# Copying the value products' whole accumulator side out of PSUM on ScalarE, and adding its halves on VectorE from SBUF

## The chip, the core and the metric

The kernel runs on one core of a Trainium2 chip. The engines named below are TensorE (PE in the profile, with its weight loads listed apart as PEld), VectorE (DVE), ScalarE (ACT), GpSimd (POOL) and SyncE (SP, which issues DMA transfers). TensorE writes its products to PSUM; the other engines read them from there or work in SBUF. The metric is the device time of one execution in microseconds.

## What is computed

One step of a hybrid decoder layer: a prompt of 1024 tokens and 8 single-token samples go through one input projection, stick-breaking attention with 16 heads of 64 channels, a state-space branch, gates, an output projection and a layer norm. The change lies in the prompt's attention, which is, cut to its core:

```python
z = jnp.einsum("bqhd,bkhd->bhqk", q, k) * (HEAD_DIM ** -0.5) + sb_bias
causal = k_pos[None, :] < q_pos[:, None]
log_beta = jax.nn.log_sigmoid(z)
log_keep = jnp.where(causal, log_beta - z, 0.0)
log_w = log_beta + lax.cumsum(log_keep, axis=3, reverse=True) - log_keep
w = jnp.where(causal, jnp.exp(log_w), 0.0)
o = jnp.einsum("bhqk,bkhd->bqhd", w, v)
...
y_att = (o * jax.nn.silu(g_att)) @ w_att_out
```

A weight w of query t and key s is beta(t, s) times the product of (1 - beta) over the keys between s and t; so the keys need a running product instead of a softmax.

## The kernel before

Heads are worked on in 8 pairs. While the attention of pair p runs, TensorE also computes the input projection of pair p + 1 (line 142, 344 columns at a time, each product three times with values split in a high and a low part), and GpSimd prepares tables for the state-space branch (lines 495 to 510). The order of TensorE's instructions is written out by the program: a list of attention steps, with projection matmuls woven in between by an assumed cost for each step. The other engines' order comes from the scheduler when the program is built; every engine then works through its own list in order and waits on semaphores.

For a head h of a pair, the queries are taken in four blocks m of 256 (two of 128 each), in the order m = 3, 0, 2, 1. For a block:

- `scores` (lines 661 to 673): TensorE makes q.k for 128 queries (z, in PSUM). ScalarE makes keep = sigmoid(-z) (ke, line 662) and beta = sigmoid(z) (be, line 663). VectorE makes the running product over the keys with a scan (line 672), and multiplies it into beta (line 673).
- `turn` (lines 690 to 694): TensorE transposes the weights of two key blocks (tp, in PSUM). ScalarE copies them out rounded as the high part (wthi, or wdhi on the diagonal, line 693), and VectorE makes the low part (wtlo, wdlo, line 694).
- `values` (line 707), two turns later (LAG = 2): TensorE multiplies with the values. The stationary operand holds the values' high part in 64 columns and their low part in the other 64, so that the result has the high part's products in partitions 0 to 63 and the low part's in 64 to 127. Four matmuls go with each turn: high, low, high, low part of the weights.

When a block's last turn is in, its result has to be read: the two halves of the partitions are added, the sum is multiplied by the attention gate, silu(g) (sg), and sent to DRAM. The accumulator is one tile `o` of PSUM with two sides of 256 columns, used by turns:

```python
self.acc, self.side = ps.tile([128, 2, 256], F32, tag="o", bufs=1, name="o"), 0
```

The first matmul of a block waits for the reading of the block just before it. That holds although the blocks alternate sides: both sides are one tile. There are 8 pairs, 2 heads and 4 blocks, so 64 such readings. In the lines that read, `own` is the half of the partitions that belongs to head h, 0 to 63 for h = 0 and 64 to 127 for h = 1. Line 714 (ScalarE) copies the low half out, line 715 (VectorE) adds the high half from PSUM, line 716 (VectorE) multiplies by the gate, line 717 sends. `high_priority` moves instructions ahead in the scheduler's choice.

Of the kernel before, what the change touches and what calls it, by code (L numbers as in the profile page):

```python
# [13 lines left out]
ALU = mybir.AluOpType  # L14
# [70 lines left out]
def blk(i, w=128):  # L85
    return slice(w * i, w * i + w)
# [454 lines left out]
class Attention:  # L541
# [155 lines left out]
    def values(self, p, h, m, j, hi, lo):  # L697

        k, nc, pool, st = self.k, self.k.nc, self.pool, self.st[p]
        first, last = ORDER[m][0], ORDER[m][-1]  # L700
        if j == first:
            self.side = 1 - self.side
        o = self.acc[:, self.side]
        for a in range(2):
            v, at = st["v"][h][:, 2 * j + a], 2 * a if j < m else 2 - 2 * a
            for t in (hi, lo):
                nc.tensor.matmul(o, v, t[:, at:at + 2].rearrange("p a b -> p (a b)"),  # L707
                                 start=(j == first and a == 0 and t is hi), stop=(j == last and a == 1 and t is lo))
        if j != last:
            return  # L710
        own = slice(64 * h, 64 * h + 64)
        x = pool.tile([128, 256], F32, tag="ox", bufs=3, name="ox")
        with k.tc.high_priority(HURRY):
            nc.scalar.copy(x[own], o[64:128])
            nc.vector.tensor_tensor(x[own], o[0:64], x[own], ALU.add)
        nc.vector.tensor_tensor(x[own], x[own], st["sg"][own, blk(m, 256)], ALU.mult)  # L716
        k.q["A"].dma_start(k.d_a[p][own, blk(m, 256)], x[own])

# [1001 lines left out]
```

## Time and profile before

| | us |
|---|---|
| median of 3 runs | 1667.35 (1664.79 to 1669.0) |
| profiled execution | 1668.55 |
| its span | 1666.5 |
| PE busy in it | 1497.7 (90%) |
| DVE busy | 1265.3 (76%) |
| POOL busy | 895.0 (54%) |
| ACT busy | 754.0 (45%) |

The span is the time from the first to the last instruction in the profiled execution. The busy time of an engine counts its instructions, not its waits. The values in a row of the timeline are the start, the duration, the engine, the line, the operation, what it writes and reads with their sizes (partitions x columns), and how many alike are put together; a bracket at the end tells how long the engine had been idle before and what ended that. An instruction of DVE or ACT can be listed as starting a little before its predecessor ends.

### The profile page before, as it was taken

How to read it: one execution, taken by the hardware profiler on the slowest of the kernel's cores; microseconds unless marked ns; L12 is line 12 of the kernel's file. 1: busy time of each engine (PE TensorE's matmuls, PEld its weight loads, DVE VectorE, ACT ScalarE, POOL GpSimd, SP SyncE). 2: the span in 40 equal slices, each digit the busy share in tenths (PEclk: the TensorE clock that was granted, in tenths of full speed). 3: DMA queues.
4: the chain of work that ended last, by engine and by line, in shares of the span. 5: the costliest groups of instructions: out<-in, count | busy, mean ns of one | idle time of the engine just before them, and what ended most of it. 6: DMA issues, size and time to landing. Idle time of an engine off the chain costs nothing.

```text
span 1666.5 us, 26016 instructions
## 1 busy us (share of the span) xinstructions
PE 1497.7 (90%) x9257; PEld 1423.4 (85%) x9257; DVE 1265.3 (76%) x2342; ACT 754.0 (45%) x1380; POOL 895.0 (54%) x744
## 2 busy tenths in 40 slices
PE   4899899999999999999989898987988869999997
PEld 3799898989898989899978888887878869999885
DVE  8748888888888888872688878978559994544566
ACT  4466666666676666663333333333352222321200
POOL 3437676767676767664456555456336542122154
PEclk8899999999999999999999999889989989999998
DMA  9233333333333333326689888768355576754322
GB/s 333 71 100 82 81 81 81 81 81 81 82 81 82 81 81 81 81 88 205 214 274 292 261 256 266 256 200 233 113 181 172 188 266 240 250 182 150 105 89 89
DMA packets 164125, 258.72 MB, mean 155 GB/s; under 512 B 45049, under 2 KB 106233, under 8 KB 163867
## 3 DMA queue, kind: packets, MB, share of 16 engines
q1 hardware_dynamic: 137945, 163.62, 32.5%
q0 software_dynamic: 23456, 84.95, 15.9%
q10 hardware_dynamic: 2594, 8.49, 1.9%
q8 instruction: 73, 1.20, 0.3%
q14 instruction: 57, 0.47, 0.1%
HBM read 188.38 MB, written 57.86 MB: 148 GB/s over the span
## 4 chain that ended last, share of the span: by engine, by line
PE 41%; DVE 25%; issue 8%; DMA 5%; ACT 4%; POOL 2%; SPq 0%; DVEq 0%; ACTq 0%; POOLq 0%
PE pj L142 26%; PE f L1403 6%; DVE l_t L895 4%; DVE s_sc L837 3%; DVE ke L672 3%; PE o L707 3%; PE tp L690 2%; DMA s_t<-in_cache_k,s_idx 2%; PE z L661 2%; DVE vs L643 2%; DVE be L673 2%; DVE s_t L832 1%; DMA w<-in_w_in 1%; DVE m L1255 1%; DVE ox L716 1%
## 5 line engine op out<-in xcount | busy, mean ns | idle before, releaser
L142 PE MATMUL pj<-ahi,whi 128*128 128x344 f32 x2112 | 700.9, 333 | 56.9 <-ACT u L981 20.4
L142 PE MATMUL pj<-alo,whi 128*128 128x344 f32 x2112 | 691.3, 329 | 10.3 <-DVE alo L1231 5.8
L142 PE MATMUL pj<-ahi,wlo 128*128 128x344 f32 x2112 | 585.0, 329 | 14.2 <-POOL wlo L110 14.2
L142 PEld LDWEIGHTS pj<-ahi,whi 128*128 128x128 f32 x2112 | 410.3, 194 | 65.6 <-ACT u L981 21.4
L142 PEld LDWEIGHTS pj<-alo,whi 128*128 128x128 f32 x2112 | 410.5, 194 | 15.3 <-DVE alo L1231 6.9
L142 PEld LDWEIGHTS pj<-ahi,wlo 128*128 128x128 f32 x2112 | 385.0, 193 | 17.6 <-POOL wlo L110 15.8
L672 DVE TENSOR_TENSOR_SCAN ke<-ke,eye 128x896 f32<-128x896 f32 (+7 forms) x128 | 214.2, 1674 | 81.9 <-ACT ke L662 81.5
L110 POOL TENSOR_TENSOR wlo<-w,whi 128x1024 fp32r<-128x1024 f32 x53 | 134.2, 2532 | 242.7 <-ACT whi L109 242.4
L109 ACT CAST whi<-w 128x1024 fp32r<-128x1024 f32 x90 | 94.9, 1055 | 162.0 <-PE pj L142 111.3
L662 ACT ACTIVATE ke<-z,nhb 128x448 f32<-128x448 f32 (+2 forms) x192 | 112.0, 583 | 82.6 <-PE z L661 79.2
L673 DVE TENSOR_TENSOR be<-be,ke 128x896 f32<-128x896 f32 (+7 forms) x128 | 128.3, 1003 | 11.7 <-DVE ke L672 0.5
L837 DVE SCALAR_TENSOR_TENSOR s_sc<-s_t,s_q,s_sc 128x512 f32<-128x512 f32 x126 | 112.4, 892 | 22.0 <-issue 9.9
L663 ACT ACTIVATE be<-z,hb 128x448 f32<-128x448 f32 (+2 forms) x192 | 110.7, 577 | 0.0
L816 POOL DMA_INDIRECT s_t<-in_cache_k,s_idx x64 | 71.3, 1114 | 39.8 <-issue 12.8
L690 PE MATMUL tp<-ident,be 128*128 128x128 f32 x576 | 89.4, 273 | 0.0
L495 POOL TENSOR_TENSOR pr<-tab 128x256 f32<-128x256 f32 x32 | 31.1, 972 | 102.4 <-DMA tab<-d_tab 98.8
L693 ACT CAST wthi<-tp 128x512 fp32r<-128x512 f32 x96 | 56.6, 590 | 54.7 <-PE tp L690 52.6
L895 DVE SCALAR_TENSOR_TENSOR l_t<-l_t,l_sc 128x128 f32<-128x128 f32 x256 | 78.5, 366 | 2.3 <-DMA l_t<-in_cache_v,l_idx 2.3
L496 POOL TENSOR_TENSOR pt<-tab 128x256 f32<-128x256 f32 x64 | 77.8, 1216 | 3.1
L574 POOL TENSOR_TENSOR sg<-sg,zg 128x1024 f32<-128x1024 f32 x8 | 22.0, 2746 | 99.2 <-ACT sgs L573 99.2
L1525 ACT ACTIVATE gate<-pj 128x344 f32<-128x344 f32 x72 | 33.0, 459 | 92.2 <-PE pj L142 90.1
L661 PE MATMUL z<-kl,qs 128*128 128x448 f32 (+2 forms) x192 | 66.7, 348 | 3.0 <-DMA kl<-kl 3.0
(320 smaller groups left out, 2865.6 us busy)
## 6 DMA issues: line engine op xcount, KB each, us to landing
w<-in_w_in SPq DMA_DIRECT2D x38, 512.0 KB
w<-in_w_in POOLq DMA_DIRECT2D x26, 512.0 KB
wc<-in_w_cond SPq DMA_DIRECT2D x24, 512.0 KB
gst<-d_gg SPq DMA_DIRECT2D x8, 576.0 KB
x<-in_xr SPq DMA_DIRECT2D x9, 512.0 KB
xt<-in_xt SPq DMA_DIRECT2D x8, 516.0 KB
d_ma<-gate SPq DMA_DIRECT2D x8, 516.0 KB
d_mm<-gate SPq DMA_DIRECT2D x8, 516.0 KB
```

The source lines that it names most:

```text
L109: nc.scalar.copy(whi, w32)
L110: self.eng.tensor_tensor(wlo, w32, whi.bitcast(F32), ALU.subtract)
L142: PE.matmul(ps[c], w[:, blk(t)], x[:, cs(c)], start=(t == 0 and i == 0), stop=(t == KT - 1 and i == 2))
L661: nc.tensor.matmul(z[:, 0:wide], st["q", h][:, blk(i)], x[:, s:s + wide], start=j == 0, stop=j == 1)
L662: nc.scalar.activation(ke[:, s:s + cw], z[:, 0:cw], AF.Sigmoid, bias=k.nhb[:, hd:hd + 1], scale=-0.125)
L663: nc.scalar.activation(be[:, s:s + cw], z[:, 0:cw], AF.Sigmoid, bias=k.hb[:, hd:hd + 1], scale=0.125)
L672: nc.vector.tensor_tensor_scan(rev, rev, self.eye[:, NP - n:][:, ::-1], 0.0, ALU.mult, ALU.add)
L673: nc.vector.tensor_tensor(be, be, ke[:, 1:n + 1], ALU.mult)
L690: PE.transpose(tp[:, 2 * order[a] + e], w[e][:, blk(2 * j + a)], k.ident)
L837: DVE.scalar_tensor_tensor(sc, t, q[:, d - d0:d - d0 + 1], sc, op0=ALU.mult, op1=ALU.add)
L895: nc.vector.scalar_tensor_tensor(t[:, d], t[:, d], 1.0, self.sc, op0=ALU.mult, op1=ALU.mult, accum_out=self.acc[:, j, 8 * c + d:8 * c + d ...
L1403: PE.matmul(pp[c], a[:, token(i)], w[:, blk(c, 512)], start=(t == 0 and a is ah and w is wh), stop=(t == KT - 1 and a is al))
```

## The change

ScalarE copies all 128 partitions of the accumulator's side, and not only its lower products; VectorE then adds the two halves of this copy in SBUF, and no longer reads PSUM. The addition is also taken out of the block with the raised priority.

```diff
         own = slice(64 * h, 64 * h + 64)
         x = pool.tile([128, 256], F32, tag="ox", bufs=3, name="ox")
         with k.tc.high_priority(HURRY):
-            nc.scalar.copy(x[own], o[64:128])
-            nc.vector.tensor_tensor(x[own], o[0:64], x[own], ALU.add)
+            nc.scalar.copy(x, o)
+        nc.vector.tensor_tensor(x[own], x[0:64], x[64:128], ALU.add)
         nc.vector.tensor_tensor(x[own], x[own], st["sg"][own, blk(m, 256)], ALU.mult)
         k.q["A"].dma_start(k.d_a[p][own, blk(m, 256)], x[own])
```

The order of the instructions is the same on every engine in the two programs; what changes is which of them wait for what. On TensorE, at the first value products of the second block (m = 0) of the first pair's first head, the program of before has these rows (the bracket names the engines whose counts are waited for):

```order
L707 MATMUL o<-wdhi,vs 128x256 [waits DVE_49]
L707 MATMUL o<-wdlo,vs 128x256
```

and the changed program these:

```order
L707 MATMUL o<-wdhi,vs 128x256 [waits Activation_49]
L707 MATMUL o<-wdlo,vs 128x256 [waits DVE_49]
```

The first matmul's wait on VectorE for line 715 of the block before (m = 3) has become one on ScalarE for line 714; and the second matmul now has a wait on VectorE of its own, for wdlo of line 694, which line 715's wait covered before.

On VectorE, where the result of that block m = 0 is read, before:

```order
L672 SCALAR_TENSOR_TENSOR ke_636<-ke_636,eye 128x1024 [waits Activation_49]
L715 TENSOR_TENSOR ox<-o,ox 64x256 [waits Activation_49]
L673 TENSOR_TENSOR be<-be,ke_636 128x1024 [waits DVE_49]
L694 TENSOR_TENSOR wdlo<-tp,wdhi 128x384 [waits Activation_49]
L716 TENSOR_TENSOR ox<-ox,sg 64x256 [waits DVE_49]
```

and changed:

```order
L672 SCALAR_TENSOR_TENSOR ke_636<-ke_636,eye 128x1024 [waits Activation_49]
L715 TENSOR_TENSOR ox<-ox 64x256 [waits Activation_49]
L673 TENSOR_TENSOR be<-be,ke_636 128x1024 [waits DVE_49]
L694 TENSOR_TENSOR wdlo<-tp,wdhi 128x384 [waits Activation_49]
L716 TENSOR_TENSOR ox<-ox,sg 64x256
```

Line 715 keeps its place. Line 716 needs no wait on its own engine any more, because the wait of line 673 now reaches up to line 715.

## Rows read from the trace of the kernel before

**Rows 1.** Busy time by stretch: length, then PE, PEld, DVE, ACT, POOL; granted clock.
```profile
125.00:770.00 645.00, 604.54 (x4001) 583.54 (x4001) 547.69 (x607) 429.94 (x857) 445.06 (x395) 0.98 0.32 83
...
423.00:443.00 20.00, 17.00 (x106) 15.85 (x106) 18.71 (x20) 12.21 (x27) 11.55 (x11) 0.91 0.41 103
443.00:464.00 21.00, 20.93 (x143) 20.56 (x142) 17.86 (x21) 15.02 (x30) 14.46 (x14) 1.00 0.17 49
```

**Rows 2.** Waits, 125 to 770 us: total us, times, longest us.
```profile
PEld o L707 <- DVE ox L715: 34.9, 32, 2.9
...
PEld o L707 <- DVE wtlo L694: 13.3, 7, 2.2
```

**Rows 3.** Timeline of PE's weight loads, 430 to 444 us: start, us, instruction, idle before.
```profile
431.16 0.19 PEld L707 LDWEIGHTS o<-wdhi,vs 128*128 128x128 f32 x1 [2.11 <-DVE ox L715]
...
437.77 0.19 PEld L707 LDWEIGHTS o<-wthi,vs 128*128 128x128 f32 x1 [1.34 <-DVE ox L715]
```

**Rows 4.** ACT's instructions by shape, 125 to 770 us: count, busy us, mean ns.
```profile
L714 ACT COPY ox<-o 64x256 f32<-64x256 f32 x64 | 23.6, 369 | 34.4 <-PE o L707 32.8
...
L571 ACT COPY sg<-pj 128x336 f32<-128x336 f32 x7 | 3.0, 432 | 0.0
```

**Rows 5.** Timeline of ACT, 425 to 433 us.
```profile
425.40 0.37 ACT L714 COPY ox<-o 64x256 f32<-64x256 f32 x1
```

**Rows 6.** Timeline of DVE, 423 to 448 us.
```profile
423.67 2.33 DVE L672 TENSOR_TENSOR_SCAN ke<-ke,eye 128x896 f32<-128x896 f32 x1 [0.97 <-ACT ke L662]
...
434.39 2.88 DVE L672 TENSOR_TENSOR_SCAN ke<-ke,eye 128x1024 f32<-128x1024 f32 x1
437.30 0.42 DVE L715 TENSOR_TENSOR ox<-o,ox 64x256 f32<-64x256 f32 x1
437.75 0.56 DVE L694 TENSOR_TENSOR wdlo<-tp,wdhi 128x384 fp32r<-128x384 f32 x1
...
440.66 0.68 DVE L694 TENSOR_TENSOR wtlo<-tp,wthi 128x512 fp32r<-128x512 f32 x1
...
443.47 0.42 DVE L715 TENSOR_TENSOR ox<-o,ox 64x256 f32<-64x256 f32 x1 [0.53 <-ACT ox L714]
```

**Rows 7.** Timeline of PE, 397 to 401 and 440 to 443 us.
```profile
400.25 0.39 PE L707 MATMUL o<-wtlo,vs 128*128 128x256 f32 x1 [1.91 <-DVE wtlo L694]
...
440.73 0.28 PE L707 MATMUL o<-wdlo,vs 128*128 128x256 f32 x1
...
442.33 0.28 PE L707 MATMUL o<-wtlo,vs 128*128 128x256 f32 x1
```

**Rows 8.** Lines 715 and 716: least, median and longest ns, first and last start.
```profile
L715 DVE TENSOR_TENSOR ox<-o,ox x64: 386/414/419, 140.8 to 765.5; 64x256 f32<-64x256 f32 x64
...
L716 DVE TENSOR_TENSOR ox<-ox,sg x64: 403/423/2153, 142.7 to 765.9; 64x256 f32<-64x256 f32 x64
```

**Rows 9.** Timeline of DVE, 384 to 402 us.
```profile
384.96 2.02 DVE L672 TENSOR_TENSOR_SCAN ke<-ke,eye 128x896 f32<-128x896 f32 x1 [2.46 <-ACT ke L662]
386.90 0.39 DVE L715 TENSOR_TENSOR ox<-o,ox 64x256 f32<-64x256 f32 x1
387.22 1.25 DVE L673 TENSOR_TENSOR be<-be,ke 128x896 f32<-128x896 f32 x1
...
392.14 0.39 DVE L715 TENSOR_TENSOR ox<-o,ox 64x256 f32<-64x256 f32 x1
...
394.16 2.15 DVE L716 TENSOR_TENSOR ox<-ox,sg 64x256 f32<-64x256 f32 x1
```

**Rows 10.** Timeline of POOL, 384 to 402 us.
```profile
385.17 2.35 POOL L497 TENSOR_TENSOR pi<-pi,pt 128x256 f32<-128x256 f32 x1
...
390.14 2.55 POOL L496 TENSOR_TENSOR pt<-cc,tab 128x288 f32<-128x288 f32 x1
...
392.77 3.27 POOL L587 TENSOR_TENSOR qs<-z,qs 64x1024 fp32r<-64x1024 f32 x1
396.11 0.87 POOL L497 TENSOR_TENSOR gi<-gi,pt 128x288 f32<-128x288 f32 x1
```

## The prediction

> **What bounds the kernel now.** I read the busy time by stretch first, then the waits, then the timeline of one head pair, 372 to 454 us; the other pairs repeat it. All 64 instances of the changed lines run in the attention stage. There, from 125 to 770 us, the reader sees TensorE (PE) busy 604.5 of 645.0 us and VectorE (DVE) 547.7 [rows 1]: PE is the longer queue, DVE is not far behind, so a wait taken from PE can come back as another wait for DVE.
>
> The waits name the line that changes: PE's weight loads (PEld) stood idle 34.9 us, 32 times, until L715 had ended, and 13.3 us, 7 times, until L694 [rows 2]. The reason is the order on DVE. L715 stands behind a scan (L672) of up to 2.88 us [rows 6], and the next value products (L707) may not write into the accumulator's bank until L715 has read it. In the pair shown the loads wait 2.11 us at 431.16 and 1.34 us at 437.77, 3.45 us together [rows 3]. Eight pairs of that are 27.6 us; the 7.3 us that are left of the list are short waits, 0.9 us a pair.
>
> **The change part by part.** *The wait goes to ScalarE.* L714 now releases the bank. In front of the 2.11 us wait it had ended at 425.40 + 0.37 = 425.77 us, 5.4 us before L715 let PE go on [rows 3, 5]. It now copies 128 partitions instead of 64, with as many columns. Its price lies between 369 ns (today's mean) and 432 ns (128x336 from PSUM: all 128 partitions and more columns) [rows 4]; I take 369, since the 63 ns between the two have 80 more columns to account for. Either end is far below those 5.4 us. PE's direct gain is up to 34.9 us.
>
> *What is late next.* The second matmul of each L707 group reads wtlo or wdlo, which DVE makes at L694. DVE's run from 423.67 to 443.47 us shows no idle time [rows 6], so an earlier PE does not make it earlier. Inside it, wdlo is ready at 437.75 + 0.56 = 438.31 and wtlo at 440.66 + 0.68 = 441.34 us, and PE reads them at 440.73 and 442.33 [rows 6, 7]. The spare is 2.42 and then 0.99 us. Of the 3.45 us that PE gains in front of them it has to give back all but 0.99; that much stays, since DVE next waits for ACT (0.53 us idle at 443.47) and ACT for PE. Of the short waits I keep half, 0.45 us a pair, because two further L715 of a pair meet GpSimd work and sit right in front of an L694. Kept: 0.99 + 0.45 = 1.44 us a pair, times 8 is 11.5 us. Its bounds are 0 and 34.9.
>
> *L715 from SBUF.* It becomes an instruction like L716: 64x256, both inputs in SBUF. L715 took at most 419 ns, L716 up to 2153, with medians of 414 and 423 [rows 8]. The timeline tells why: L716 at 394.16 lay beside a GpSimd (POOL) tensor_tensor that ran from 392.77 to 396.04 and ended 0.27 us behind it, while L715, with one input in PSUM, passed beside POOL's at 386.90 and 392.14 in 0.39 us [rows 9, 10]. The price of one L715 lies between 0 and 2.15 - 0.42 = 1.73 us. I price these two as L716, done 0.28 us behind the POOL instruction that they meet: POOL ends at 385.17 + 2.35 = 387.52 and at 390.14 + 2.55 = 392.69, so L715 ends at 387.80 and not 387.29, and at 392.97 and not 392.53 [rows 9, 10]. That is 0.51 and 0.44 us.
>
> [...]
>
> *Two small losses in order.* The program now lets L673 behind L715 wait for L715 and not for the scan alone (the order rows show L716's own wait on DVE gone for that). Today L673 starts 0.07 us before L715 has ended (387.22 against 387.29) [rows 9]. And L715 now reads two halves of the partitions: where its output lies in the lower half, it starts today 0.08 us before the scan has ended (386.90 against 386.98), where it lies in the upper, 0.03 behind (437.30 against 434.39 + 2.88) [rows 6, 9]. I take 0.03 behind for both: 0.11 for L715 and 0.10 for L673, twice, 0.42 us a pair. Bounds: 0 and twice that.
>
> Both L715 of this stretch lie in a DVE run from 384.96 to beyond 400 us that ends in the L694 for which PE already waits 1.91 us at 400.25 [rows 7, 9]. So all of it comes out on PE: 0.51 + 0.44 + 0.42 = 1.37 us a pair, times 8 is 11.0 us. Bounds: 0, and 8 x 2 x 1.73 = 27.7.
>
> **The sum.** -11.5 + 11.0 = -0.5 us on the profiled execution's 1668.55 us (span 1666.5 and 2.05 around it), which lies 1.2 above the median of the three runs, 1667.35. I give the forecast on the median: 1666.9 us. What the stage gains or loses I carry to the end undiminished, as PE is the queue that goes through it.
>
> **The rivals.** *Faster: POOL hardly touches L715* (chance 0.23). For it: the POOL instructions that L715 meets are themselves drawn out by the scan in front (2.35 and 2.55 us; one of their kind took 0.87 at 396.11 [rows 10]), so they may end sooner than their rows say. Then 0.42 x 8 = 3.4 us stand against 11.5 (15.1 with the short waits kept whole): 8 to 12 us faster, 1656 to 1659. Within it, with 0.02, DVE gives way altogether and the full 34.9 come: 1632; the spares of 2.42 and 0.99 us speak against it.
>
> *Slower, by a GpSimd instruction that slips in* (0.20). L673 used to stand ready while L715 ran. Now it waits for L715's end, and by then POOL's next tensor_tensor is already waiting and goes first; L673 waits for it as L716 did. One such instruction takes 0.87 us [rows 10]; two a pair in 8 pairs are 13.9 us: 1681. It decides once more than 0.3 us per instance come in this way (16 x 0.3 = 5). Against it: POOL then has that work behind it and hinders DVE less later in the same run. [...]
>
> *Slower, by the clock* (0.15). [...]
>
> **How the numbers follow.** What a measurement of this kernel can tell from no change is 0.3%, 5 us. The forecast, chance 0.42, with its own range from 1662 to 1672, is no change. Faster by more: 0.23. Slower by more: 0.20 + 0.15 = 0.35. The range from 1657 to 1680 takes in most of the faster rival and the lower part of the slower ones, and leaves out 2 in 10.
>
> **What would show it.** Right: no wait of PE for L715; in its place longer waits for L694 (13.3 us on PEld becoming some 44: 11.0 more at places like 400.25, and 8 x 2.46 given back at places like 438 and 441); the two L715 of a pair that meet POOL at 0.8 to 1 us; L714 at 370 ns. Wrong: L715 at 0.42 us throughout (then the faster rival), L673 grown by more than L715 (POOL first), or a granted clock below 1 in the busy stretch behind 443 us of a pair (the clock). If PE's idle time in the stage falls by over 10 us, the claim that DVE takes back the gain is wrong.

## The result, and the profile after

The changed kernel takes 1681.8 us (median of 7 runs, 1674.15 to 1683.79) against 1666.35 us before (7 runs): ratio 1.0088, 95% interval 1.0069 to 1.0107. It is slower by 15 us. The forecast was no change, 1666.9 us, and the range ended at 1680. The profiled execution took 1683.79 us, span 1682.0.

The attention stage first. The stretch is drawn out to 790 us because the stage ends later; columns as in [rows 1], then PE's waits as in [rows 2]:

```profile
125.00:790.00 665.00, 608.03 (x3997) 590.71 (x3996) 568.92 (x607) 427.90 (x857) 456.11 (x394) 0.97 0.31 80
```

```profile
PEld o L707 <- DVE wtlo L694: 34.9, 15, 4.1
...
PEld tps L621 <- DVE wtlo L694: 17.6, 7, 2.7
...
PEld o L707 <- DVE wdlo L694: 7.8, 10, 1.2
```

The wait for L715 is gone from the list, all 34.9 us of it. In its place stand 60.3 us of waits for L694, where there had been 13.3 [rows 2]. 17.6 us of them are on a line that did not wait before at all, L621. VectorE needs 568.92 us for the 607 instructions that took 547.69 [rows 1]: 21.2 us more for the same work.

Where on VectorE? The groups by shape (count, busy us, mean ns, idle before), and the two lines' least, median and longest:

```profile
L715 DVE TENSOR_TENSOR ox<-ox 64x256 f32<-64x256 f32 x64 | 44.2, 690 | 5.0 <-ACT ox L714 3.1
L716 DVE TENSOR_TENSOR ox<-ox,sg 64x256 f32<-64x256 f32 x64 | 36.2, 566 | 1.1
...
L673 DVE TENSOR_TENSOR be<-be,ke 128x1024 f32<-128x1024 f32 x15 | 29.8, 1988 | 0.3
```

```profile
L715 DVE TENSOR_TENSOR ox<-ox x64: 420/670/2490, 140.7 to 786.0; 64x256 f32<-64x256 f32 x64
L716 DVE TENSOR_TENSOR ox<-ox,sg x64: 404/423/2150, 143.5 to 786.4; 64x256 f32<-64x256 f32 x64
```

L715's median went from 414 to 670 ns [rows 8], and its last instance from 765.5 to 786.0 us: the stage ends 20.5 us later, of which some 5 are made up behind it. L673 of 128x1024 takes 1988 ns on the mean, though nothing in it was edited; before it was

```profile
L673 DVE TENSOR_TENSOR be<-be,ke 128x1024 f32<-128x1024 f32 x15 | 19.5, 1297 | 0.1
```

One pair shows why. These are VectorE and GpSimd in the stretch that answers to [rows 9, 10], some 6 us later than there:

```profile
391.36 2.51 DVE L672 TENSOR_TENSOR_SCAN ke<-ke,eye 128x896 f32<-128x896 f32 x1 [1.95 <-ACT ke L662]
393.90 0.79 DVE L715 TENSOR_TENSOR ox<-ox 64x256 f32<-64x256 f32 x1
394.72 1.46 DVE L673 TENSOR_TENSOR be<-be,ke 128x896 f32<-128x896 f32 x1
...
399.35 0.73 DVE L715 TENSOR_TENSOR ox<-ox 64x256 f32<-64x256 f32 x1
400.12 3.31 DVE L673 TENSOR_TENSOR be<-be,ke 128x1024 f32<-128x1024 f32 x1
...
403.81 0.54 DVE L716 TENSOR_TENSOR ox<-ox,sg 64x256 f32<-64x256 f32 x1
404.28 2.60 DVE L672 TENSOR_TENSOR_SCAN ke<-ke,eye 128x128 f32<-128x128 f32 x1
...
409.08 0.68 DVE L694 TENSOR_TENSOR wtlo<-tp,wthi 128x512 fp32r<-128x512 f32 x1
```

```profile
399.88 2.46 POOL L587 TENSOR_TENSOR qs<-z,qs 64x1024 fp32r<-64x1024 f32 x1
```

L715 ends at 400.08, and L673 starts 0.04 us later. But GpSimd's L587 was already up, at 399.88; it runs until 402.34, and L673 ends at 403.43. In the kernel before these were VectorE's rows at the same place, between those of [rows 9]:

```profile
392.45 1.32 DVE L673 TENSOR_TENSOR be<-be,ke 128x1024 f32<-128x1024 f32 x1
...
396.24 1.02 DVE L672 TENSOR_TENSOR_SCAN ke<-ke,eye 128x128 f32<-128x128 f32 x1
```

There L673 started 0.08 us ahead of the end of L715 (392.45 against 392.53); L587 was up only at 392.77 [rows 10] and met L716 instead. From the start of the scan at 391.36 to the end of wtlo at 409.76 are 18.40 us; the same run of instructions took 384.96 to 400.19, 15.23 us. I call this run A (first head of a pair: from the 128x896 scan to the wtlo behind the 128x128 product). PE stands at its end:

```profile
403.95 0.39 PE L707 MATMUL o<-wdlo,vs 128*128 128x256 f32 x1 [0.97 <-DVE wdlo L694]
409.82 0.39 PE L707 MATMUL o<-wtlo,vs 128*128 128x256 f32 x1 [3.86 <-DVE wtlo L694]
...
443.54 0.49 PE L621 MATMUL tps<-ident,zs 128*8 128x128 f32 x3 [2.50 <-DVE wtlo L694]
```

The 1.91 us wait of [rows 7] has become 3.86, with 0.97 in front of it. Behind it TensorE's granted clock was 0.66 on the mean (0.50 from 412 to 414 us, 1.00 again from 415 us), while PE was busy throughout (columns as in [rows 1]):

```profile
410.00:415.00 5.00, 5.00 (x26) 4.94 (x27) 3.74 (x7) 2.49 (x5) 0.00 (x0) 0.66 0.78 206
```

At 443.54 the 2.11 us of [rows 3] are back, as 2.50 us, on L621. The transposes of sample_rows write into a buffer of the turned weights, and cannot start before L694 has read it. In the profile before, these two rows (VectorE, PE) show that they had 0.41 us to spare, 432.24 - (431.14 + 0.69):

```profile
431.14 0.69 DVE L694 TENSOR_TENSOR wtlo<-tp,wthi 128x512 fp32r<-128x512 f32 x1
```

```profile
432.24 0.55 PE L621 MATMUL tps<-ident,zs 128*8 128x128 f32 x3
```

### The profile page after: what moved, and what is told of

Read it like the earlier page. It is cut to its first block, busy times and chain, and to the rows that moved or that the text cites. A ratio compares the mean times of both kernels' runs of the same rounds, so it can differ in the third digit from the quotient of the medians.

```text
span 1682.0 us, 26015 instructions
## 1 busy us (share of the span) xinstructions
PE 1501.7 (89%) x9257; PEld 1431.1 (85%) x9257; DVE 1291.7 (77%) x2342; ACT 752.5 (45%) x1380; POOL 904.7 (54%) x744
## 4 chain that ended last, share of the span: by engine, by line
PE 48%; DVE 25%; DMA 7%; issue 7%; ACT 5%; SPq 2%; POOL 2%; DVEq 0%; ACTq 0%; POOLq 0%
PE pj L142 32%; PE f L1403 6%; DVE ke L672 4%; DVE l_t L895 4%; DVE be L673 3%; PE o L707 3%; PE z L661 2%; PE tp L690 2%; DVE vs L643 2%; DMA w<-in_w_in 1%; DVE ox L715 1%; DVE s_sc L837 1%; DMA d_g<-yy 1%; DVE wtlo L694 1%; DVE ox L716 1%
## 5 line engine op out<-in xcount | busy, mean ns | idle before, releaser
L673 DVE TENSOR_TENSOR be<-be,ke 128x896 f32<-128x896 f32 (+7 forms) x128 | 134.0, 1047 | 12.2 <-ACT wthi L693 0.5
L663 ACT ACTIVATE be<-z,hb 128x448 f32<-128x448 f32 (+2 forms) x192 | 110.8, 577 | 0.0
L816 POOL DMA_INDIRECT s_t<-in_cache_k,s_idx x64 | 70.0, 1093 | 38.9 <-issue 12.5
L495 POOL TENSOR_TENSOR pr<-tab 128x256 f32<-128x256 f32 x32 | 27.0, 844 | 116.6 <-DMA tab<-d_tab 112.9
L707 PE MATMUL o<-wtlo,vs 128*128 128x256 f32 x192 | 52.7, 296 | 31.2 <-DVE wtlo L694 31.0
L496 POOL TENSOR_TENSOR pt<-tab 128x256 f32<-128x256 f32 x64 | 78.7, 1229 | 3.1
```

Source lines behind the costliest of these rows:

```text
L663: nc.scalar.activation(be[:, s:s + cw], z[:, 0:cw], AF.Sigmoid, bias=k.hb[:, hd:hd + 1], scale=0.125)
L673: nc.vector.tensor_tensor(be, be, ke[:, 1:n + 1], ALU.mult)
```

## The experiments

Theory H, formed on this: the sum of two SBUF inputs that lie in different partitions makes VectorE stop twice, in front of L715 and behind it, and GpSimd's tensor_tensor gets in at these stops. A stop means that an instruction starts a little behind the end of the one in front, and not ahead of it; the expectations below also call it a hold. Rivals: the order on VectorE costs the time without GpSimd (B); the wait on L621 does (M); ScalarE's wider copy does.

Beside each time stands the ratio to the kernel before on the same chip, with its 95% interval. For the runs that bear on it I also give the length of VectorE's runs A, added up over the 8 pairs (before 116.7 us, after 135.8), read from its timeline; run B is the same run for the second head (7 of them, before 122.5, after 127.0). The runs were on several chips, so two of them are compared by their ratios where the times are close.

**GpSimd's part, taken away from both (e1, e2).**

```
-        t1 = sp.tile(shape, F32, tag="pt", bufs=1, name="pt")
-        POOL.tensor_tensor(dst, a, b, ALU.mult)
-        POOL.tensor_tensor(t1, c, d, ALU.mult)
-        POOL.tensor_tensor(dst, dst, t1, op)
+        POOL.memset(dst, 0.0)
```

> The kernel before, with the three GpSimd tensor_tensor of each complex product (L495 to L497: phasors, inputs and outputs of the SSM tables) replaced by one memset, so that the tables are zero; the other GpSimd work (L574, L587, L613) stays. It is the base for the run beside it. Theory A (GpSimd and the new SBUF sum exclude each other): VectorE's instructions with two SBUF inputs get shorter here too; L716's mean falls from 643 ns towards 430, and the whole gets 5 to 15 us faster than 1667. Theory B (the order on VectorE alone, GpSimd does not matter): within 5 us of the kernel before.

> The changed kernel with the same GpSimd work left out (tables zero). Compared with the run of before that leaves out the same. Theory A (contention with GpSimd makes the change slow): L715's mean falls from 690 ns to below 500, L673 128x1024 from 1988 to below 1500 ns, and the change now costs nothing or gains: 0 to 15 us faster than the other. Theory B (order: L673 waiting for L715, wtlo queued behind L715, L621 waiting for L694): the change still costs 8 to 20 us.

Measured: 1617.68 us (0.9741, 0.972 to 0.9762) without the change, 1612.36 us (0.9693, 0.9665 to 0.9721) with it. With little GpSimd work the change costs nothing; it looks 5 us faster, though the two intervals just touch. Theory B falls. L673 behind the sum is nearly back, L715 only in part (changed kernel, e2):

```profile
L715 DVE TENSOR_TENSOR ox<-ox 64x256 f32<-64x256 f32 x64 | 37.2, 580 | 7.7 <-ACT ox L714 6.0
...
L673 DVE TENSOR_TENSOR be<-be,ke 128x1024 f32<-128x1024 f32 x15 | 20.4, 1362 | 0.3
```

I had expected L715 below 500 ns; it is 580, beside the GpSimd work that stays. In e1 L716's mean is 511 ns, not near 430. Expected of e1 were 5 to 15 us, and it gained 44: GpSimd's table work costs the kernel before far more than this change is about. The attention stage ends 46 us earlier there: the last L715 starts at 719.0 us instead of 765.5.

**The wider copy alone (e3).**

```
-        nc.vector.tensor_tensor(x[own], x[0:64], x[64:128], ALU.add)
+        nc.vector.tensor_tensor(x[own], o[0:64], x[64:128], ALU.add)
```

> The changed kernel, but VectorE's sum takes its lower half from PSUM as before (o[0:64] + x[64:128]), so the bank is again released by L715; ScalarE's copy stays at the whole 128 partitions. Theory A and B alike: the copy itself costs nothing, 1663 to 1671 us, L715 back at 0.41 us, L673 128x1024 at 1.30 us, PE's wait for L715 back at some 35 us. If instead the 128-partition copy on ScalarE is what costs: over 1675 us.

Measured: 1664.66 us (1.002, 1.0006 to 1.0034), runs A 115.8 us, L715 417 ns, PE's wait for L715 43.5 us. The 128-partition copy is not what costs.

This run shows one thing more. Its sum reads one input from the upper partitions in SBUF, and both stops are there: in runs A L715 starts 0.03 us behind the scan and L673 0.03 us behind L715. VectorE and GpSimd in the pair shown, the first L715 behind a scan that ends at 394.46:

```profile
394.50 0.42 DVE L715 TENSOR_TENSOR ox<-o,ox 64x256 f32<-64x256 f32 x1
394.95 1.09 DVE L673 TENSOR_TENSOR be<-be,ke 128x896 f32<-128x896 f32 x1
...
399.82 0.42 DVE L715 TENSOR_TENSOR ox<-o,ox 64x256 f32<-64x256 f32 x1
400.26 1.23 DVE L673 TENSOR_TENSOR be<-be,ke 128x1024 f32<-128x1024 f32 x1
```

```profile
397.71 2.55 POOL L496 TENSOR_TENSOR pt<-cc,tab 128x288 f32<-128x288 f32 x1
400.34 3.40 POOL L587 TENSOR_TENSOR qs<-z,qs 64x1024 fp32r<-64x1024 f32 x1
```

Nothing is lost. Beside a sum with one input in PSUM GpSimd's L496 ran to its end at 400.26, and its next instruction was up 0.08 us too late. So in this run the stops alone cost nothing (runs A 115.8 us, 116.7 before); as I read it, one costs when a GpSimd instruction is already up. In the changed kernel the sum itself meets GpSimd, and the next one was up 0.24 us before L673.

**The stops, undone and put back (e4, e5).** In e4 ScalarE makes two copies of 64 partitions, into the same partitions of two tiles; in e5 each copy stays in its own. The rest is equal, to the order on every engine. Both have two ox tiles and one oy, where the changed kernel has three ox.

```
 e4: nc.scalar.copy(x[own], o[64:128]); nc.scalar.copy(y[own], o[0:64])
     nc.vector.tensor_tensor(x[own], y[own], x[own], ALU.add)
 e5: nc.scalar.copy(x[64:128], o[64:128]); nc.scalar.copy(y[0:64], o[0:64])
     nc.vector.tensor_tensor(x[own], y[0:64], x[64:128], ALU.add)
```

> The changed kernel, but ScalarE copies the two halves with two instructions into the same 64 partitions of two tiles, and VectorE adds them there: the sum still has both inputs in SBUF and the bank is still released by ScalarE, but L716 waits for L715 by a semaphore again, so L673 behind an L715 does not wait for it, and L715 reads one set of partitions. In one place a pair L694 (wdlo) now stands behind L673 instead of in front of it. Theory A with slip-in through L673's wait (GpSimd gets in because L673 is held): L673 128x1024 falls back from 1988 to about 1300 ns and some 10 us of the 15 come back: 1668 to 1674. Theory A without it (any SBUF sum meets GpSimd): still 1678 to 1686. ScalarE's extra 64 copies of 0.37 us may add a little.

> As the run with two ScalarE copies into the same partitions (e4), with the same instructions in the same order on every engine, but each copy stays in its own partitions (0 to 63 and 64 to 127), so the sum again reads two sets of partitions: L715 starts only when VectorE's instruction in front has ended, and what follows it starts only when L715 has ended. Nothing but this differs from e4. Theory H (the two holds let GpSimd in between, and that is the loss): 1676 to 1684 us, L673 128x1024 back at 1.8 us and more, the starts 0.03 us behind the end in front instead of 0.08 us before it. Theory O (what made e4 as fast as before is the one L694 that moved behind L673, or the second copy on ScalarE, not the holds): 1663 to 1668 us.

Measured: e4 1665.07 us (1.0018, 1.0001 to 1.0036), e5 1678.44 us (1.0097, 1.0062 to 1.0132). e4 came out better than I had expected, e5 as theory H has it. The 13 us between them come with the partitions alone, and so with the stops. TensorE's granted clock in the stage is 0.97 in both. VectorE in run A with one GpSimd instruction, e4 first, then e5:

```profile
386.13 2.02 DVE L672 TENSOR_TENSOR_SCAN ke<-ke,eye 128x896 f32<-128x896 f32 x1 [1.94 <-ACT ke L662]
388.07 0.78 DVE L715 TENSOR_TENSOR ox<-oy,ox 64x256 f32<-64x256 f32 x1
388.78 1.07 DVE L673 TENSOR_TENSOR be<-be,ke 128x896 f32<-128x896 f32 x1
...
392.92 0.83 DVE L715 TENSOR_TENSOR ox<-oy,ox 64x256 f32<-64x256 f32 x1
393.67 1.21 DVE L673 TENSOR_TENSOR be<-be,ke 128x1024 f32<-128x1024 f32 x1
...
398.92 0.68 DVE L694 TENSOR_TENSOR wtlo<-tp,wthi 128x512 fp32r<-128x512 f32 x1
```

```profile
393.55 2.00 POOL L497 TENSOR_TENSOR gr<-gr,pt 128x288 f32<-128x288 f32 x1
```

```profile
389.76 2.02 DVE L672 TENSOR_TENSOR_SCAN ke<-ke,eye 128x896 f32<-128x896 f32 x1 [1.93 <-ACT ke L662]
391.82 0.67 DVE L715 TENSOR_TENSOR ox<-oy,ox 64x256 f32<-64x256 f32 x1
392.52 1.52 DVE L673 TENSOR_TENSOR be<-be,ke 128x896 f32<-128x896 f32 x1
...
397.20 0.86 DVE L715 TENSOR_TENSOR ox<-oy,ox 64x256 f32<-64x256 f32 x1
398.09 1.59 DVE L673 TENSOR_TENSOR be<-be,ke 128x1024 f32<-128x1024 f32 x1
...
405.38 0.68 DVE L694 TENSOR_TENSOR wtlo<-tp,wthi 128x512 fp32r<-128x512 f32 x1
```

```profile
397.85 0.75 POOL L496 TENSOR_TENSOR pt<-cc,tab 128x288 f32<-128x288 f32 x1
```

In e4 L673 starts 0.08 us ahead of the end of L715 (393.67 against 393.75) and takes 1.21 us; in e5 0.03 behind it, and takes 1.59 here, 3.3 in three other pairs. In both GpSimd's next instruction is up before L673 starts, by 0.12 us in e4 and 0.24 in e5. In e4 L673 is done first all the same, at 394.88, and L497 lasts 2.00 us; in e5 GpSimd is done first, at 398.60, and L673 ends 1.08 us behind it. So being up first in these rows does not decide it; what differs is the stop. Run A is 13.47 us against 16.30 in this pair, 108.6 against 129.7 us in all. L715 itself is no measure of the loss: it meets GpSimd in e4 too and is longer there, 849 ns against 667, and VectorE's busy time in the stage is about the same (565.19 us in e4, 569.14 in e5, from 125 to 790 us). What the stops decide, as I read it, is where the two meet: at an instruction with time to spare, or in the run for which PE waits. Which of the two stops costs how much was not tried apart; of the 21.1 us between the runs A, L673 behind L715 has about 11.

That e4 is no faster than the kernel before, though its runs A are 8 us shorter, lies with other waits: PE's loads wait 16.2 us at L661 for ScalarE's L663 (3.5 before), beside 14.4 us at L621 and 19.4 at L707 for L694. The second copies on ScalarE alone do not make the first of these: e5 has them too, and waits 4.4 us there.

In the second head of a pair the result lies in the upper partitions, and there L715 starts 0.03 us behind the end of its predecessor in the kernel before too [rows 6]. Runs B differ by 0.2 us between e4 and e5 (125.9, 126.1).

Among the starts of the stage that I read one by one, those with no idle time in front, L715 starts ahead of the end in front in 28 of 45 places in e4, mostly by 0.07 or 0.08 us, and in none of 48 in e5, where it is 0.02 to 0.04 us behind; L673 next to an L715 starts ahead in 14 of 18 places in e4 and in none of 18 in e5. In the changed kernel the wait of L673 for L715 is one that the program sets. Why VectorE starts behind where the inputs lie in two sets of partitions was not shown.

**The same pair with little GpSimd work (e9, e10).** e4 and e5 with the edit of e1.

> e4 (both copies into the same partitions, so no hold) with the GpSimd work of the SSM tables left out as in e1 and e2 (tables zero). With the next run it gives the price of the holds where GpSimd has little to slip in. Theory H (a hold costs only what GpSimd does in the gap): 1608 to 1614 us, within 4 us of the next run. Theory B (the hold itself costs VectorE the time, some 13 us as between e4 and e5): 10 us or more faster than the next run.

> e5 (each copy in its own partitions, so L715 and what follows it are held) with the same GpSimd work left out; the instructions and their order are those of the run before it. Theory H: 1608 to 1616 us, within 4 us of it, with L673 128x1024 at 1.2 to 1.4 us. Theory B: 1620 us or more.

Measured: 1614.56 us (0.9706, 0.9676 to 0.9735) and 1611.76 us (0.9689, 0.9659 to 0.972): no difference. Runs A are 99.2 and 102.0 us, 2.8 apart and not 21.1. So a stop costs here what GpSimd does in it: from 125 to 790 us GpSimd is busy 179.0 us in e9 and 187.8 in e10, against 474.9 in e4 and 458.3 in e5. Together with e3 to e5 that settles H.

**L621 (e6, e7).** The changed kernel, and e4, with the transposes in another PSUM buffer:

```
-        tp = self.ps.tile([128, 512], F32, tag="wt", name="tps")
+        tp = self.ps.tile([128, 512], F32, tag="z", name="tps")
```

> The changed kernel, but the transposes of L621 write into a PSUM buffer of the scores (z) and not into one of the turned weights (wt), so they no longer wait for L694. Theory M (the step that my sum missed: the wait for L715 came back as a wait of L621 for L694): the 17.6 us of PE's wait at L621 go, and part of it stays gone: 1670 to 1677 us. Theory D (VectorE sets the pace anyway, so the wait only moves on to the next L707): within 4 us of the changed kernel, 1678 to 1685, with L707's wait for L694 grown by about what L621 lost.

> e4 (two ScalarE copies into the same partitions, no hold) together with L621's transposes in a z buffer. In e4 PE waits 14.4 us at L621. If early release is worth something once both losses are gone: 1652 to 1662 us, faster than both kernels. If VectorE or ScalarE takes it back: 1663 to 1668 us.

Measured: 1685.27 us (1.0148, 1.0112 to 1.0183) and 1672.89 us (1.0054, 1.003 to 1.0078). Theory M falls. The wait at L621 is gone, and L707's for wdlo has grown from 7.8 to 26.6 us (e6):

```profile
PEld o L707 <- DVE wtlo L694: 34.7, 14, 4.1
PEld o L707 <- DVE wdlo L694: 26.6, 12, 3.3
```

VectorE is late there, whichever of PE's lines notices it first. By the ratios e6 is even some 10 us slower than the changed kernel, and e7 some 6 slower than e4, where the two intervals overlap; in e7 PE waits 28.1 us for wdlo. Why the move costs time I did not find out.

**Is the early release worth anything? (e11, e15)** In e11 only the two value products of a pair that wait long are released by ScalarE, without a stop:

```
-        x = pool.tile([128, 256], F32, tag="ox", bufs=3, name="ox")
+        x, y = (pool.tile([128, 256], F32, tag=n, bufs=b, name=n) for n, b in (("ox", 2), ("oy", 1)))
         with k.tc.high_priority(HURRY):
             nc.scalar.copy(x[own], o[64:128])
-            nc.vector.tensor_tensor(x[own], o[0:64], x[own], ALU.add)
+            low = o[0:64]
+            if h == 1 and m in (3, 0):
+                low = y[own]
+                nc.scalar.copy(low, o[0:64])
+            nc.vector.tensor_tensor(x[own], low, x[own], ALU.add)
```

> The kernel before, with e4's two copies into the same partitions only for the two value products of a pair in front of whose release PE waits long (h = 1, query blocks 3 and 0: the 2.11 and 1.34 us of the pair shown); the other six of a pair keep the sum from PSUM. In one place a pair wdlo stands behind L673, as in e4. If the early release is worth the spare of wtlo alone (0.99 us a pair, 8 us) and the two sums pay 0.3 us each: 1658 to 1663 us. If L621's wait for L694 and the moved wdlo take it back: 1662 to 1668 us, no change. Slower than 1670 only if wdlo behind L673 comes out on PE in full.

Measured: 1662.27 us (0.9987, 0.9971 to 1.0003), no difference that can be told. PE's waits (L719 is L715 here):

```profile
PEld tps L621 <- DVE wtlo L694: 16.7, 7, 2.6
PEld o L707 <- DVE wtlo L694: 14.0, 10, 2.1
PEld o L707 <- DVE ox L719: 9.3, 18, 0.9
PEld o L707 <- DVE wdlo L694: 1.6, 1, 1.6
```

25.6 of the 34.9 us for the sum are gone, and 16.7 are back at L621.

> e4 with three ox and two oy tiles instead of two and one (the room comes from rs, which now takes an sv tile); same instructions in the same order. In e4 ScalarE waited 9.2 us in the attention stage for these tiles, and PE 16.2 us for ScalarE. If the kept gain of the early release (11.5 us in my sum) is there and was hidden by that: 1650 to 1660 us, faster than before. If VectorE and ScalarE have no room anyway: 1662 to 1667 us.

Measured: 1665.61 us (1.0025, 1.0007 to 1.0043), as e4. It does not answer its question: taking rs out of its own buffer made ScalarE wait 39.8 us for the DMA of sv, and PE 22.0 us for that.

**VectorE relieved (e8, e12, e13, e14, e16).** In e12 one word of the kernel before is changed, and the gate product runs on GpSimd:

```
-        nc.vector.tensor_tensor(x[own], x[own], st["sg"][own, blk(m, 256)], ALU.mult)
+        nc.gpsimd.tensor_tensor(x[own], x[own], st["sg"][own, blk(m, 256)], ALU.mult)
```

> The kernel before, with the gate product (L716) as a GpSimd tensor_tensor; VectorE loses 41.2 us of busy time in the attention stage, GpSimd gains 64 instructions. If VectorE's queue binds PE there: PE's wait for L715 falls by half and more, 1640 to 1655 us. If the two engines' instructions with two SBUF inputs exclude each other wherever they stand: the same work meets L673 now, 1660 to 1670 us.

> The changed kernel with the gate product (L716) on GpSimd, as in e12. L715 still reads two sets of partitions, so the holds are there, and GpSimd has more that can slip in. If the holds with GpSimd's full work are what makes the change slow: slower than e12 (1632) by 8 to 20 us, 1640 to 1652. If VectorE, with 41 us less to do, has room for them and the early release then gains: 1622 to 1632 us.

Measured: e12 1631.89 us (0.9804, 0.9773 to 0.9835), faster than the kernel before by some 2% and faster than I had expected either way; e13, the change on top of it, 1636.38 us (0.9852, 0.9835 to 0.9868). The stretch (the last L715 starts at 736.5 us here), the product on GpSimd and PE's wait in e12:

```profile
125.00:790.00 665.00, 642.68 (x4322) 621.70 (x4321) 543.82 (x588) 445.48 (x888) 536.51 (x485) 1.00 0.37 100
```

```profile
L716 POOL TENSOR_TENSOR ox<-ox,sg 64x256 f32<-64x256 f32 x64 | 75.5, 1188 | 23.9 <-DVE ox L715 19.7 <-PE pj L142 2.5
```

```profile
PEld o L707 <- DVE ox L715: 30.1, 37, 2.2
```

The 75.5 us on GpSimd are no loss: no engine's wait in the stage names a gate product. The wait for L715 hardly falls, against what I had expected; what goes is the wait for L694 (13.3 us before) and the lower clock (granted 0.98 before, 1.00 now), with runs A at 96.6 and B at 115.3 us. e13 costs 4.5 us more, or 8 by the ratios, with runs A at 106.6: the stops are still there (L715 and the L673 behind it start 0.02 to 0.04 us behind the end in front). That is at the lower edge of what I had expected from them, and that the two differ is not certain, as their intervals touch.

Three runs told less than they were meant to, each for a buffer that was too small or was shared. All have e4's copies; in e8 the sum and the gate product run on GpSimd, in e14 and e16 the gate product alone.

> e4's two ScalarE copies into the same partitions, with the sum and the gate product (L715, L716) as GpSimd tensor_tensor instead of VectorE's. VectorE loses 128 instructions, some 80 us busy in the attention stage, GpSimd gains as many. If VectorE's queue is what binds PE here: PE's waits for L694 fall below 15 us and the kernel takes 1640 to 1655 us. If what counts is the work that needs two SBUF inputs on either engine (they exclude each other): GpSimd's extra instructions hold up VectorE's L673 instead, 1660 to 1670 us.

Measured: 1752.97 us (1.054, 1.0511 to 1.0569). ScalarE's second copy waited 149.0 us for the one oy tile, which GpSimd had not read yet, and PE behind it.

> e4 (two ScalarE copies into the same partitions, sum of two SBUF inputs without a hold, early release) with the gate product on GpSimd. If the early release is worth something once VectorE has room and nothing is held: up to the 30 us that PE still waits for L715 in e12, so 1605 to 1628 us, the fastest. If ScalarE's 64 further copies, or the sums that now meet GpSimd's gate products, take it back: 1628 to 1636 us, the same as e12.

Measured: 1692.16 us (1.0178, 1.0156 to 1.02); ScalarE waited 40.8 us for an ox tile whose DMA had not left.

> e14 with three ox and two oy tiles. In e14 ScalarE's copies waited 40.8 us for an ox tile until its DMA had left, since the gate products on GpSimd come late. If that wait was what made e14 slow: 1605 to 1632 us; below 1627 the early release gains where VectorE has room, around 1632 it gives nothing beside e12. If ScalarE's further copies are the cause: still over 1660 us.

Measured: 1671.38 us (1.0058, 1.0037 to 1.0078). Its further tiles are paid for with rs as in e15: ScalarE waited 59.2 us and PE 48.5. So an early release without a stop beside e12 has not been tried fairly.

## Why the prediction was wrong

- *The direct gain of 34.9 us and L714's price*: right. The wait is gone; L714 takes 372 ns on the mean, 369 had been taken. One reading was wrong: in front of the first of the two L715 of that stretch stand two L643, 3.38 us together, and not a scan; the wait behind it is the same.
- *Kept: 0.99 + 0.45 us a pair, 11.5 in all*: this step failed. I looked for what is late next among the value products alone and read spares of 2.42 and 0.99 us there [rows 6, 7]. L621 stands in front of both with 0.41 us. e11, which has this gain nearly alone, shows 2 us, not told from none. Moving L621 does not bring it (e6), so the spare of wdlo was not there either: the runs B that make wdlo and wtlo had become 4.6 us longer. Where VectorE has much more room, e2 against e1, about 5 us may be kept, which is not clear of the noise.
- *L715 from SBUF, 0.51 + 0.44 us a pair*: right in size. The two of the pair shown took 0.79 and 0.73 us where they had taken 0.39 each, 0.74 more together. What I had not seen is that L715's own length says little about the time (e4).
- *Two small losses in order, 0.42 us a pair*: this is the step that made the sum wrong. I counted the stops at 0.03 us behind instead of 0.07 ahead, which they are to a hundredth, and not what gets in through them. Runs A grew by 19.1 us; the two stretched L715 make about 6 of it (8 x 0.74), the rest, 13, is 1.7 us a pair where the sum has 0.42. The 13 us of the whole kernel between e4 and e5 are of the same size.
- *The rival "a GpSimd instruction that slips in"*, chance 0.20, 13.9 us, 1681: this is what happened. That its figure is met is luck in part: it has 16 instructions of 0.87 us, while in runs A L673 grew by 12.5 us, 10.4 of them in the 128x1024 product alone (some 2 us in each of five pairs), and its 1681 still holds the 11.5 us kept that did not come. What I held against it, that GpSimd would hinder VectorE less later, came true and was undone in the same run: in the pair shown L716 took 0.54 us instead of 2.15, but the scan of 128 columns 2.60 instead of 1.02. VectorE's busy time grew, too. I could have given the rival more: [rows 9, 10] show GpSimd's L587 getting in ahead of L716 for 1.7 us.
- *The clock*, a chance of 0.15 by my estimate: a small part, and at another place. Behind 443 us of the pair shown it was 1.00. But behind the wait of 3.86 us it was 0.66 from 410 to 415 us, with PE busy throughout. The stage has 0.97 where it had 0.98 [rows 1]. What a fall of the clock alone costs no run shows; from PE's busy time I estimate it: 608.03 us against 604.54 for nearly as many matmuls, 3.5 of the 20.5 us. The rest is waiting. The fall comes behind a wait that the stops made longer, and e4 and e5 differ without it.
- *"What I lose I carry to the end undiminished"*: not quite. Of 20.5 us at the end of the stage 15 are left at the end.

## What to carry to other kernels

When an edit takes PSUM out of a VectorE instruction, ask two things of what comes in: which partitions its SBUF inputs lie in (13 us between e4 and e5), and what GpSimd does at that moment (with little of its work the same two, e9 and e10, are not told apart). Behind a stop of a few hundredths of a microsecond in VectorE's queue L673 took 3.31 us in the pair shown, with a GpSimd instruction already up, and 1.23 where none was yet (e3). And when a wait is removed, look for the next late thing among all instructions that follow on that engine, those of other stages too, not among the kin of the one that waited.

## What had not been expected of the hardware

- In the changed kernel L715, 64x256 with both inputs in SBUF, took 0.42 us where no GpSimd instruction ran (at 193.48 us) and 2.49 us at 266.92, beside GpSimd's tensor_tensor L613 from 266.69 to 269.13; L673's 128x1024 product in the pair shown took 3.31 us, and 1.21 in e4.
- The same two stops in VectorE's queue cost nothing around a sum with one input in PSUM (e3: 1664.66 us, runs A 115.8 against 116.7 us).
- Leaving out GpSimd's table arithmetic made the kernel before 44 us faster (0.9741), without one instruction less on PE, VectorE or ScalarE; yet giving GpSimd 64 gate products more, which took 41.2 us off VectorE, made it 32 us faster (e12). With the same GpSimd work, the partitions of VectorE's inputs alone made 13 us (e4 against e5).
